# Split SiLU-multiply: loads on SP, stores on ACT, and one wide activation and multiply per tile

## The chip, the cores and the metric

One core of one Trainium2 chip runs the kernel. The metric is the device time of one execution in microseconds (us), as a median over runs. A page or a trace shows one profiled execution; its span is about 2 us shorter than the device time of the same execution (468.9 against 470.65 us for the kernel before).

Engines: ACT is ScalarE, DVE is VectorE, SP is SyncE, which here only issues transfers. A "q" after the name (SPq, ACTq, DVEq) means that engine's sequencer. 16 DMA engines move the data.

## The reference

```python
def setup_inputs():
    batch, seq, dim = (32, 512, 2048)
    return {'x': np.random.randn(batch, seq, dim).astype(np.float32)}

def reference(x):
    half_dim = x.shape[-1] // 2
    x1, x2 = (x[..., :half_dim].copy(), x[..., half_dim:].copy())
    silu_x1 = x1 * (1 / (1 + np.exp(-x1)))
    return (silu_x1 * x2).astype(np.float32)
```

134.22 MB have to be read and 67.11 MB written. Per element of output there is one SiLU and one multiply.

## The kernel before

The 16384 rows are cut into 16 tiles of 1024 rows. Each of the 128 partitions holds 8 rows of a tile, so a load is 8.39 MB and a store 4.19 MB. There are two input buffers and two output buffers. Tile i+2 can be loaded only when the last multiply of tile i has read its input.

```python
K = 8
KC = 2
in_pool  = ...tile_pool(name="in_pool", bufs=2)
out_pool = ...tile_pool(name="out_pool", bufs=2)
# ... cut ...
def load(i):
    xt = in_pool.tile([P, K, in_cols], dt, name="xt")
    nc.scalar.dma_start(out=xt[:, :plan[i][1], :], in_=view(x_flat, i))   # loads: ACT queue
    loaded[i] = xt

load(0)
load(1)
for i in range(n_tiles):
    # ... cut ...
    for c in range(0, k, KC):                     # 4 chunks of 2 rows
        ce = min(c + KC, k)
        nc.scalar.activation(out=ot[:, c:ce, :], in_=xt[:, c:ce, :half], func=Silu)
        nc.vector.tensor_mul(out=ot[:, c:ce, :], in0=ot[:, c:ce, :], in1=xt[:, c:ce, half:])
        if last:
            nc.sync.dma_start(out=ov[:, c:ce, :], in_=ot[:, c:ce, :])      # stores: SP queue
    if not last:
        nc.sync.dma_start(out=ov, in_=ot[:, :k, :])
    if i + 2 < n_tiles:
        load(i + 2)
```

With four chunks, the activation of one chunk runs beside the multiply of the chunk before.

Of the kernel before, what the change touches and what calls it, by code (L numbers as in the profile page):

```python
# [1 line left out]

# [4 lines left out]


def issue_ahead_of_the_first_barrier(nc):




    head, body = nc.main_func.blocks[:2]
    load = next(ins for ins in body.instructions if type(ins).__name__ == "InstDMACopy")
    at = next(
        j for j, ins in enumerate(head.instructions)
        if ins.engine == load.engine and type(ins).__name__ == "InstDrain"
    )
    body.instructions = [ins for ins in body.instructions if ins.name != load.name]  # L20
    head.instructions = head.instructions[:at] + [load] + head.instructions[at:]


@with_exitstack
def kernel(
    ctx: ExitStack,
    tc: tile.TileContext,
    x: bass.AP,
    out: bass.AP,
):  # L30






    nc = tc.nc
    P = nc.NUM_PARTITIONS

    x_flat = x.flatten_outer_dims()  # L40
    out_flat = out.flatten_outer_dims()
    num_rows, in_cols = x_flat.shape
    half = in_cols // 2
    dt = x_flat.dtype

    K = 8
    KC = 2
    PLAN = [K] * (num_rows // (P * K))

    in_pool = ctx.enter_context(tc.tile_pool(name="in_pool", bufs=2))  # L50
    out_pool = ctx.enter_context(tc.tile_pool(name="out_pool", bufs=2))

    plan = []
    row = 0
    for k in PLAN:
        plan.append((row, k))
        row += P * k
    assert row == num_rows
    n_tiles = len(plan)

    def view(flat, i):
        row0, k = plan[i]
        return flat[row0:row0 + P * k].rearrange("(p k) d -> p k d", k=k)

    nc.at_finalize(issue_ahead_of_the_first_barrier)


    ctx.enter_context(tc.manual_schedule())

    loaded = {}  # L70

    def load(i):
        xt = in_pool.tile([P, K, in_cols], dt, name="xt")
        nc.scalar.dma_start(out=xt[:, :plan[i][1], :], in_=view(x_flat, i))
        loaded[i] = xt

    load(0)
    load(1)
    for i in range(n_tiles):
        k = plan[i][1]  # L80
        xt = loaded.pop(i)
        last = i == n_tiles - 1
        ov = view(out_flat, i)
        ot = out_pool.tile([P, K, half], dt, name="ot")
        for c in range(0, k, KC):
            ce = min(c + KC, k)
            nc.scalar.activation(  # L87
                out=ot[:, c:ce, :],
                in_=xt[:, c:ce, :half],
                func=mybir.ActivationFunctionType.Silu,  # L90
            )
            nc.vector.tensor_mul(  # L92
                out=ot[:, c:ce, :],
                in0=ot[:, c:ce, :],
                in1=xt[:, c:ce, half:],
            )
            if last:
                nc.sync.dma_start(out=ov[:, c:ce, :], in_=ot[:, c:ce, :])
        if not last:
            nc.sync.dma_start(out=ov, in_=ot[:, :k, :])  # L100
        if i + 2 < n_tiles:
            load(i + 2)


# [1 line left out]
_INS = ['x']  # L106
_OUTS = [((32, 512, 1024), 'float32')]


# [23 lines left out]
```

## Time and profile before

| | before |
|---|---|
| device time, median of 3 runs before the prediction | 470.82 us |
| bytes moved, mean rate | 201.35 MB, 429 GB/s |
| DVE busy, ACT busy | 30%, 25% |
| from arrival of a tile's load to the issue of its store and of the next load but one | 10.87 us |
| arrival to arrival | 29.0 us |

These lines are from the page of the kernel before. In part 3, a row is a queue with its packets, its bytes, and its packets' time as a share of 16 engines' span. In part 5, the columns are busy time and mean length of one instruction, then the idle time before and its releaser. In part 6, the last column is the median time from issue to landing.

```profile
span 468.9 us, 269 instructions
DVE 142.3 (30%) x64; ACT 118.2 (25%) x65; POOL 0.2 (0%) x4
q10 hardware_dynamic: 2304, 134.22, 66.4%
q1 hardware_dynamic: 2736, 67.11, 33.2%
...
DMA xt<-in_x_dram 80%; DVE ot L92 15%; ACT ot L87 3%; DVEq L128 0%
...
L92 DVE TENSOR_TENSOR ot<-ot,xt 128x2048 f32<-128x2048 f32 x64 | 142.3, 2286 | 319.5 <-ACT ot L87 319.5
L87 ACT ACTIVATE ot<-xt 128x2048 f32<-128x2048 f32 x64 | 116.9, 1897 | 338.8 <-DMA xt<-in_x_dram 338.8
...
out_dram<-ot SPq DMA_DIRECT2D x15, 4096.0 KB, 39.8
xt<-in_x_dram ACTq DMA_DIRECT2D x16, 47.1
```

The two queues' packets fill 66.4 + 33.2 = 99.6% of the 16 engines' time. Compute engines stand idle most of the time, waiting for a load.

Three rows of the table by stretches follow. The columns are the stretch in us, its length, busy time of DVE, ACT and POOL, the clock, the DMA share and GB/s. The first two rows are two tiles each in the middle; the last is part of the finish, after the last load has arrived. A packet is counted whole in the stretch in which it starts, so short stretches scatter around 434 GB/s.

```profile
44.50:102.60 58.10, 17.79 (x8) 14.62 (x8) 0.00 (x0) 1.00 1.00 433
102.60:160.60 58.00, 17.79 (x8) 14.63 (x9) 0.00 (x0) 1.00 1.00 434
...
455.00:458.00 3.00, 3.00 (x3) 3.00 (x2) 0.00 (x0) 1.00 0.76 325
```

This is one link of the chain of waits, in order of time (start, length, what):

```profile
44.54 1.92 ACT ot L87
...
46.48 8.91 DVE ot L92 x4
...
55.41 47.19 DMA xt<-in_x_dram
```

The load is on the chain for 47.19 us. A tile of 12.58 MB (8.39 in, 4.19 out) takes only 29.0 us at 434 GB/s. For the other 18 us that load stood behind the load issued before it.

The finish, in order of time (start, length, what):

```profile
451.03 7.31 ACT L87 ACTIVATE ot<-xt 128x2048 f32<-128x2048 f32 x4 [21.57 <-DMA xt<-in_x_dram]
455.29 6.94 SPq L98 DMA_DIRECT2D out_dram<-ot  x4
```

Stores of the last tile start leaving 4.26 us after its arrival. What is left of the store before them covers that time.

### The profile page before, as it was taken

The page shows a single profiled execution, that of the slowest core. Times are in us where ns is not written, and L with a number is a line of the kernel's source. Part 1 is how long each engine was busy: PE and PEld are TensorE (multiplying, and loading weights), DVE is VectorE, ACT ScalarE, POOL GpSimd, SP SyncE. Part 2 cuts the span into 40 slices and gives each one's busy share as a digit, 9 for nine tenths or more (in the row PEclk, how much of TensorE's full clock was granted, in tenths as well). Part 3 has the DMA queues.
Part 4 walks back from the last instruction along what each step waited for, and adds up shares of the span by engine and source line. Part 5 has one row for each costly group of instructions (what it writes and reads, how often), then busy time and mean ns, then how long its engine had stood idle before and what let it go on. Part 6 is the DMA issues. An engine that isn't in the chain of part 4 may idle for free.

```text
span 468.9 us, 269 instructions
## 1 busy us (share of the span) xinstructions
DVE 142.3 (30%) x64; ACT 118.2 (25%) x65; POOL 0.2 (0%) x4
## 2 busy tenths in 40 slices
DVE  0070705106061160601507025070250702407034
ACT  1142406023060330603206032060420604106051
POOL 0000000000000000000000000000000000000000
DMA  9899999999999998999999999999999989999998
GB/s 431 375 447 403 447 447 447 403 419 431 447 447 403 447 492 363 442 492 391 458 403 439 456 447 403 409 442 447 447 403 444 467 386 447 442 419 481 400 409 354
DMA packets 5042, 201.35 MB, mean 429 GB/s; under 512 B 560, under 2 KB 560, under 8 KB 560
## 3 DMA queue, kind: packets, MB, share of 16 engines
q10 hardware_dynamic: 2304, 134.22, 66.4%
q1 hardware_dynamic: 2736, 67.11, 33.2%
q14 instruction: 2, 0.02, 0.0%
HBM read 134.22 MB, written 67.11 MB: 429 GB/s over the span
## 4 chain that ended last, share of the span: by engine, by line
DMA 80%; DVE 15%; ACT 3%; DVEq 0%; issue 0%
DMA xt<-in_x_dram 80%; DVE ot L92 15%; ACT ot L87 3%; DVEq L128 0%
## 5 line engine op out<-in xcount | busy, mean ns | idle before, releaser
L92 DVE TENSOR_TENSOR ot<-ot,xt 128x2048 f32<-128x2048 f32 x64 | 142.3, 2286 | 319.5 <-ACT ot L87 319.5
L87 ACT ACTIVATE ot<-xt 128x2048 f32<-128x2048 f32 x64 | 116.9, 1897 | 338.8 <-DMA xt<-in_x_dram 338.8
L87 ACT ACT_TABLE_LOAD x1 | 1.3, 1283 | 1.3 <-PEq L117 1.3
L117 POOL MEMSET const-uint8-127<- 128x1 uint8 x1 | 0.1, 102 | 0.0
L117 POOL MEMSET const-bfloat16-1.0<- 128x1 bf16 x1 | 0.1, 101 | 0.0
L117 POOL MEMSET const-float32-0.0<- 128x1 f32 x1 | 0.1, 98 | 0.2 <-issue 0.2
L117 POOL MEMSET const-float32-1.0<- 128x1 f32 x1 | 0.1, 98 | 0.0
## 6 DMA issues: line engine op xcount, KB each, us to landing
out_dram<-ot SPq DMA_DIRECT2D x15, 4096.0 KB, 39.8
out_dram<-ot SPq DMA_DIRECT2D x4, 1024.0 KB, 5.7
xt<-in_x_dram ACTq DMA_DIRECT2D x16, 47.1
```

What stands on the lines that cost most here:

```text
L87: nc.scalar.activation(out=ot[:, c:ce, :], in_=xt[:, c:ce, :half], func=mybir.ActivationFunctionType.Silu,)
L92: nc.vector.tensor_mul(out=ot[:, c:ce, :], in0=ot[:, c:ce, :], in1=xt[:, c:ce, half:],)
L117: nc = _bacc.Bacc("TRN2", target_bir_lowering=False, num_devices=1)
```

## The change

The intent is fewer, larger instructions: one activation and one multiply over all 8 rows in tiles 1 to 14, so 22 of each instead of 64. The queues are exchanged: loads go out from SP, stores from ACT. Tiles 0 and 15 keep chunks of 2 rows. In the last tile the store of a chunk stands two chunks behind in ACT's program, so that its wait for the multiply does not hold back the next activations.

```diff
-        nc.scalar.dma_start(out=xt[:, :plan[i][1], :], in_=view(x_flat, i))
+        nc.sync.dma_start(out=xt[:, :plan[i][1], :], in_=view(x_flat, i))
 # ... cut: silu() and mul() wrap the same activation and multiply ...
-        for c in range(0, k, KC):
-            # activation, tensor_mul of 2 rows; in the last tile a store of 2 rows on nc.sync
-        if not last:
-            nc.sync.dma_start(out=ov, in_=ot[:, :k, :])
-        if i + 2 < n_tiles:
-            load(i + 2)
+        if i < n_tiles - 1:
+            kc = KC_EDGE if i == 0 else K
+            for c in range(0, K, kc):
+                silu(ot, xt, c, c + kc)
+                mul(ot, xt, c, c + kc)
+            nc.scalar.dma_start(out=ov, in_=ot)
+            if i + 2 < n_tiles:
+                load(i + 2)
+            continue
+        cuts = list(range(0, K, KC_EDGE))
+        for n, c in enumerate(cuts + [None, None]):
+            if c is not None:
+                silu(ot, xt, c, c + KC_EDGE)
+                mul(ot, xt, c, c + KC_EDGE)
+            if n >= 2:
+                b = cuts[n - 2]
+                nc.scalar.dma_start(out=ov[:, b:b + KC_EDGE, :], in_=ot[:, b:b + KC_EDGE, :])
```

More of the change, by code (lines that the diff above doesn't have):

```diff
@@ L46 @@
     K = 8
-    KC = 2
+    KC_EDGE = 2
     PLAN = [K] * (num_rows // (P * K))
@@ L73, in load, with silu, mul @@
         xt = in_pool.tile([P, K, in_cols], dt, name="xt")
-        nc.scalar.dma_start(out=xt[:, :plan[i][1], :], in_=view(x_flat, i))
+        nc.sync.dma_start(out=xt[:, :plan[i][1], :], in_=view(x_flat, i))
         loaded[i] = xt
+    def silu(ot, xt, c, ce):
+        nc.scalar.activation(
+            out=ot[:, c:ce, :],
+            in_=xt[:, c:ce, :half],
+            func=mybir.ActivationFunctionType.Silu,
+        )
+    def mul(ot, xt, c, ce):
+        nc.vector.tensor_mul(
+            out=ot[:, c:ce, :],
+            in0=ot[:, c:ce, :],
+            in1=xt[:, c:ce, half:],
+        )
     load(0)
@@ L79 @@
     for i in range(n_tiles):
-        k = plan[i][1]
         xt = loaded.pop(i)
-        last = i == n_tiles - 1
         ov = view(out_flat, i)
         ot = out_pool.tile([P, K, half], dt, name="ot")
-        for c in range(0, k, KC):
-            ce = min(c + KC, k)
-            nc.scalar.activation(
-                out=ot[:, c:ce, :],
-                in_=xt[:, c:ce, :half],
-                func=mybir.ActivationFunctionType.Silu,
-            )
-            nc.vector.tensor_mul(
-                out=ot[:, c:ce, :],
-                in0=ot[:, c:ce, :],
-                in1=xt[:, c:ce, half:],
-            )
-            if last:
-                nc.sync.dma_start(out=ov[:, c:ce, :], in_=ot[:, c:ce, :])
-        if not last:
-            nc.sync.dma_start(out=ov, in_=ot[:, :k, :])
-        if i + 2 < n_tiles:
-            load(i + 2)
+        if i < n_tiles - 1:
[15 more added lines that the diff above has]
+                nc.scalar.dma_start(out=ov[:, b:b + KC_EDGE, :], in_=ot[:, b:b + KC_EDGE, :])
 _INS = ['x']
```

## The prediction

> **What bounds the kernel now.** The 16 DMA engines, over the whole span. The queue table shows 134.22 MB loaded and 67.11 MB stored, 429 GB/s over the 468.9 us span; the stretches between the arrivals of odd-numbered loads (chain of waits: every 58.0 us) moved 433 to 434 GB/s at a DMA share of 1.00. DVE is busy 30% and ACT 25%. The chain of waits gives compute 18%, but it is not exposed: while tile i is computed (10.9 us), load i+1 and an older store keep the engines full. The Trainium skill, "DMA: Bandwidth & Descriptors", section "Where 436 GB/s comes from", gives 435 GB/s as the ceiling of the 16 ports; the trace's 434 agrees. 201.3 MB at 434 GB/s is 464 us.
>
> **The slack.** Loads arrive every 29.05 us. A load is issued 10.9 us after the arrival two before it, 18.1 us before its predecessor has landed. A store takes 39.8 us from issue to landing, 10.7 more than the period: when it is issued the store queue still holds about 10.7 us of the store before.
>
> **What the change does.**
> 1. Tiles 1 to 14: one activation of 128x8192, then one multiply of 128x8192, no longer overlapped. Measured: 1.893 us per activation of 2048 columns, 2.284 us per multiply. The skill, "ScalarE: Activation LUTs", section "What ACT_TABLE_LOAD costs", gives 186 ns + 0.833 ns per column, which is 1.892 us at 2048 and so agrees; at 8192 it gives 7.01 us. The multiply by a similar split (estimate, 0.15 us fixed plus four times the rest): 8.7 us. So load to issue goes from 10.9 to 15.7 us, 4.8 later.
> 2. The delay fits into the slack of both queues: 18.1 to 13.3 us for loads, 10.7 to 5.9 us for stores. Neither runs dry, so loads still arrive every 29.05 us. Issue to landing should shrink by the same 4.8 us: loads 47.1 to about 42.3, stores 39.8 to about 35.0.
> 3. Swapping the queues moves the waits to other sequencers; issues cost 0.33 to 0.37 us each, all hidden. At the start the first load leaves from SP instead of ACT: within 0.3 us.
> 4. Last tile: before, its first store is issued 4.3 us after the last load landed (451.0 to 455.3), and the remains of store 14 (about 2.5 MB after 451 us, 6 us) cover that. Now this store stands behind three activations on ACT (about 5.7 us) and may leave up to 1.5 us later, while store 14 has no more left than before: 0 to 1.3 us of DMA idleness, say 0.3.
>
> **On the critical path:** only step 4 and the start. I expect 471.0 us, 80% range 470.0 to 472.3: the same within 2%.
>
> **Right or wrong.** Step 1: one activation near 7.0 us, one multiply near 8.7, in the groups. Step 2: median landings 42 and 35 us; arrivals every 29.05 us; DMA share 1.00 in the middle. Step 4: first store of the last tile 4.3 to 5.8 us after the last arrival; DMA gap before it at most 1.5 us.
>
> **What would make it wrong:** the two queues not sharing alike once swapped; store 14 finishing before the last tile's stores start; a different rate for another mixture of reads and writes. Each is worth a few us at most, so more than 9 us either way is very unlikely.

## The result, and the profile after

| | before | after |
|---|---|---|
| device time, median (range) of 6 runs each | 470.94 (470.62 to 471.61) us | 470.64 (470.44 to 471.34) us |
| ratio after/before, 95% interval | | 0.9994 (0.9981 to 1.0007) |
| span of the profiled run | 468.9 us | 468.6 us |
| arrival to issue, tiles 1 to 14 | 10.87 us | 15.78 us |
| arrival to arrival | 29.0 us | 29.0 us |

A ratio in this document is the mean time of one kernel's fast runs over that of the other's of the same rounds, so it is not quite the ratio of the medians quoted. Executions over 1.5% slower than the fastest of the same kernel are left out of the means. The result is the same time: the interval includes 1.

The page after, the same lines:

```profile
span 468.6 us, 183 instructions
DVE 139.5 (30%) x22; ACT 114.3 (24%) x23; POOL 0.2 (0%) x4
q1 hardware_dynamic: 2304, 134.22, 66.4%
q10 hardware_dynamic: 2736, 67.11, 33.2%
...
DMA xt<-in_x_dram 72%; DVE ot L85 14%; ACT ot L78 11%; DVEq L140 0%; ACTq L78 0%
...
out_dram<-ot ACTq DMA_DIRECT2D x15, 4096.0 KB, 34.7
xt<-in_x_dram SPq DMA_DIRECT2D x16, 42.1
```

Busy time fell by 2.8 us on DVE and 3.9 us on ACT, and nothing came of it. Landings fell by the 5 us by which the issues came later. On the chain of waits compute rose from 18% to 25%, about 33 us more, in the same total time: a share of the chain is not a cost.

Lengths of single instructions (shortest, median, longest in ns) by the tile view of the output:

```profile
L78 ACT ACTIVATE ot<-xt x22: 1893/7029/7029, 21.8 to 456.1; 128x8192 f32<-128x8192 f32 x14, 128x2048 f32<-128x2048 f32 x8
L85 DVE TENSOR_TENSOR ot<-ot,xt x22: 2283/8691/8693, 23.8 to 459.3; 128x8192 f32<-128x8192 f32 x14, 128x2048 f32<-128x2048 f32 x8
```

The same stretches, and one link of the chain:

```profile
44.50:102.60 58.10, 17.38 (x2) 14.06 (x2) 0.00 (x0) 1.00 1.00 433
102.60:160.60 58.00, 17.39 (x2) 14.06 (x2) 0.00 (x0) 1.00 1.00 434
...
455.00:458.00 3.00, 3.00 (x2) 3.00 (x2) 0.00 (x0) 1.00 0.78 333
```

```profile
44.84 7.04 ACT ot L78
...
51.90 8.70 DVE ot L85
...
60.62 42.14 DMA xt<-in_x_dram
```

The link now has 15.8 us of compute and 42.1 us of load, where it had 10.9 and 47.2. Its sum, 58.0 us for two tiles, has not moved, and neither have the DMA share of 1.00 and the 433 to 434 GB/s.

The finish, in order of time:

```profile
450.73 5.51 ACT L78 ACTIVATE ot<-xt 128x2048 f32<-128x2048 f32 x3 [21.93 <-DMA xt<-in_x_dram]
...
455.00 0.34 ACTq L114 DMA_DIRECT2D out_dram<-ot  x1
456.15 1.89 ACT L78 ACTIVATE ot<-xt 128x2048 f32<-128x2048 f32 x1
```

The first store left 4.27 us after the arrival, against 4.26 before. It left while the third activation was still running (until 450.73 + 5.51 = 456.24 us): the sequencer does not wait for the activations ahead of the store to finish. The Trainium skill, "Perfetto Trace Analysis", section "Sequencer Loop", says that a sequencer pushes engine instructions into a queue and reads on; this trace agrees.

### The profile page after: what moved, and what is told of

It is laid out like the page before. It is cut to its first block, busy times and chain, and to the rows that moved or that the text cites. A ratio compares the mean times of both kernels' runs of the same rounds, so it can differ in the third digit from the quotient of the medians.

```text
span 468.6 us, 183 instructions
## 1 busy us (share of the span) xinstructions
DVE 139.5 (30%) x22; ACT 114.3 (24%) x23; POOL 0.2 (0%) x4
## 3 DMA queue, kind: packets, MB, share of 16 engines
q1 hardware_dynamic: 2304, 134.22, 66.4%
## 4 chain that ended last, share of the span: by engine, by line
DMA 72%; DVE 14%; ACT 11%; DVEq 0%; issue 0%; ACTq 0%
DMA xt<-in_x_dram 72%; DVE ot L85 14%; ACT ot L78 11%; DVEq L140 0%; ACTq L78 0%
## 5 line engine op out<-in xcount | busy, mean ns | idle before, releaser
L85 DVE TENSOR_TENSOR ot<-ot,xt 128x8192 f32<-128x8192 f32 (+1 forms) x22 | 139.5, 6362 | 322.1 <-ACT ot L78 322.1
L78 ACT ACTIVATE ot<-xt 128x8192 f32<-128x8192 f32 (+1 forms) x22 | 113.0, 5163 | 343.0 <-DMA xt<-in_x_dram 343.0
## 6 DMA issues: line engine op xcount, KB each, us to landing
out_dram<-ot ACTq DMA_DIRECT2D x15, 4096.0 KB, 34.7
xt<-in_x_dram SPq DMA_DIRECT2D x16, 42.1
```

## The experiments

The main theory, "slack": the DMA engines set the time, and arrival to issue may grow a good deal in the middle for nothing; only start and finish count. The rivals were "chain" (compute between arrival and issue costs its length in each two-tile link, and something hides that) and "two effects cancel" (one part of the change gains what the other loses). All kernels ran beside runs of the kernel before on the same chip. The runs were made in four batches, each on another chip of the same kind (swap_only, wide_only, act_x2 and act_x3; thin and the three of start and finish; act_x2h and act_x4; act_x2q); the kernel before took 470.8 to 471.0 us on all four. Medians in the summary are of 4 runs, or 5 for the first two; those of act_x2 and act_x3 include one slow run each. The second and third columns are read from each profiled run; that of act_x3 alone counts as slow. The second is counted from the start of a tile's first activation, the third is a mean over tiles in the middle.

| kernel | arrival to issue | us a tile | time, us | before, us | ratio to before (95%) |
|---|---|---|---|---|---|
| swap_only | 10.9 | 29.0 | 471.05 | 470.99 | 1.0002 (0.9990 to 1.0015) |
| wide_only | 15.8 | 29.0 | 471.59 | 470.99 | 1.0008 (0.9995 to 1.0020) |
| thin (wrong result) | 2.3 | 29.0 | 471.53 | 470.98 | 1.0012 (0.9997 to 1.0027) |
| act_x2 | 22.8 | 29.0 | 470.90 | 470.99 | 0.9996 (0.9978 to 1.0014) |
| act_x2q | 24.8 | 30.5 | 494.66 | 471.00 | 1.0506 (1.0489 to 1.0524) |
| act_x2h | 26.5 | 31.3 | 501.52 | 470.81 | 1.0633 (1.0590 to 1.0675) |
| act_x3 | 29.9 | 31.9 | 513.72 | 470.99 | 1.0864 (1.0806 to 1.0922) |
| act_x4 | 37.0 | 37.4 | 592.73 | 470.81 | 1.2585 (1.2564 to 1.2606) |
| first_wide | 15.8 | 29.0 | 471.19 | 470.98 | 1.0003 (0.9988 to 1.0018) |
| last_wide | 15.8 | 29.0 | 480.75 | 470.98 | 1.0208 (1.0191 to 1.0225) |
| no_lag | 15.8 | 29.0 | 475.83 | 470.98 | 1.0105 (1.0090 to 1.0120) |

### The two parts alone

swap_only takes the changed kernel and keeps chunks of 2 rows in all tiles:

```diff
-            kc = KC_EDGE if i == 0 else K
+            kc = KC_EDGE
```

> Loads on SP, stores on ACT and the last tile's order as after, but small ops everywhere. Slack theory: load to issue stays 10.9 us, landings stay 47 us (loads) and 39.7 us (stores), time within 0.6 us of before (470.9). Rival 'two effects cancel' (the queue swap gains what the wide ops lose): faster than before by 2 us or more.

Measured: ratio 1.0002, landings 47.0 us (loads) and 39.6 us (stores):

```profile
out_dram<-ot ACTq DMA_DIRECT2D x15, 4096.0 KB, 39.6
...
xt<-in_x_dram SPq DMA_DIRECT2D x16, 47.0
```

The exchange of queues alone does nothing. The Trainium skill, "DMA: Bandwidth & Descriptors", section "Issuing engines are not separate DMA queues", says that transfers from either engine run on the same 16 DMA engines and interleave; this run agrees.

wide_only takes the kernel before, with its queues and its last tile, and makes tiles 1 to 14 wide:

```diff
-        for c in range(0, k, KC):
-            ce = min(c + KC, k)
+        kc = KC if i == 0 or last else K      # KC is 2, K is 8
+        for c in range(0, k, kc):
+            ce = min(c + kc, k)
```

> Wide activation and multiply in tiles 1 to 14, queues and last tile as before. Slack theory: landings 42.1 and 34.7 us as after, loads still 29.0 us apart, time within 0.6 us of before. Rival 'the chain of waits is right': 4.8 us later in each of its seven two-tile links is slower by up to 34 us. Rival 'two effects cancel': slower than before by 2 us or more.

Measured: ratio 1.0008, landings 42.2 and 34.7 us:

```profile
out_dram<-ot SPq DMA_DIRECT2D x15, 4096.0 KB, 34.7
...
xt<-in_x_dram ACTq DMA_DIRECT2D x16, 42.2
```

Two effects that cancel are ruled out at the size of 2 us: each part alone is within 0.2% of the kernel before at the far end of its interval. The chain's 34 us are ruled out as well.

### Compute almost taken away

thin makes all transfers of the changed kernel but computes 128 of 1024 columns. Both output tiles are filled with zeros once at the start. Its output is wrong, which doesn't matter for the time.

```diff
+    ots = [...]                 # two output tiles, memset to 0.0, reused as ots[i % 2]
-            out=ot[:, c:ce, :], in_=xt[:, c:ce, :half], func=Silu
+            out=ot[:, c:ce, :THIN], in_=xt[:, c:ce, :THIN], func=Silu      # THIN = 128
-            out=ot[:, c:ce, :], in0=ot[:, c:ce, :], in1=xt[:, c:ce, half:]
+            out=ot[:, c:ce, :THIN], in0=ot[:, c:ce, :THIN], in1=xt[:, c:ce, half:half + THIN]
```

> All transfers of the changed kernel, but only 128 of 1024 columns are computed (wrong result on purpose; the out tiles are filled with zeros once at the start): arrival to issue about 3 us instead of 15.8. Slack theory: nothing to gain, the transfers alone take this time: within 1 us of after, load landings about 55 us after issue. Rival 'compute is on the chain': about 13 us less in each of seven links, 80 us or more faster.

Measured: ratio 1.0012; arrivals every 29.0 us; loads land 55.6 us after issue. One stretch of two tiles and the loads:

```profile
102.60:160.60 58.00, 2.45 (x2) 2.11 (x2) 0.00 (x0) 1.00 1.00 433
```

```profile
xt<-in_x_dram SPq DMA_DIRECT2D x16, 55.6
```

With 2.3 us instead of 15.8 between arrival and issue, the loads only wait longer behind each other. This is the most direct evidence for the bound: with DVE busy for 34 us (20 of multiplies, 14 of fills) instead of 139, the time is the same. The rate in the middle was 433 to 434 GB/s with full and with almost no compute. The Trainium skill, "SBUF — State Buffer", section "Who interferes with whom", says that DMA never contends with a compute engine, and nothing here speaks against it.

### More compute: where does the slack end?

The changed kernel with its wide activation repeated into the same place, so that the result stays correct. act_x2, act_x3 and act_x4 run it 2, 3 and 4 times:

```diff
                 silu(ot, xt, c, c + kc)
+                if i > 0:
+                    for _ in range(1):           # range(2), range(3) in act_x3, act_x4
+                        silu(ot, xt, c, c + kc)
                 mul(ot, xt, c, c + kc)
```

> The changed kernel with each wide activation of tiles 1 to 14 run twice (same values, result unchanged): arrival to issue 15.8 + 6.9 = 22.7 us. Slack theory: still under the 29.0 us between arrivals, so loads never starve; the store queue (5.7 us of backlog) runs dry, which costs nothing while loads flow: within 1 us of after, loads landing about 35 us after issue. Rival 'chain': 7 links of 6.9 us, about 48 us slower.

Measured: ratio 0.9996, though ACT was busy for 213 us instead of 114. Loads landed 35.0 us after issue, as expected. The chain theory's 48 us did not appear. The store queue did run dry once, at the start (the first store landed at 66.5 us, the second was issued at 67.9 us), at no cost. In act_x2, act_x2q, act_x2h and first_wide most activations wait last for the store of two tiles before, which must leave its output buffer first and lands about 0.2 us after the load; more output buffers were not tried. One of the four runs took 486.2 us, at an undiminished clock. It counts as slow, was not profiled, and stays unexplained; whether act_x2 stands so near the end of the slack that it sometimes loses time is not shown.

> Each wide activation run three times: arrival to issue 29.6 us, just over the 29.0 us between arrivals. Slack theory: the knee is passed; in every second tile both queues run dry for some us. Estimate from 434 GB/s, two thirds to loads, 2 us to start a transfer: about 27 us slower than after (10 to 40), DMA share visibly under 1 in the middle. Rival 'chain': about 97 us slower.

Measured: 513.72 us; the three fast runs are 41 us over before, just outside the expected 10 to 40. (The 2 us to start a transfer are an estimate. For scale: load 0 of the kernel before landed 21.7 us after its issue, where 8.39 MB take 19.3 us at 434 GB/s.) The four runs scatter from 507.81 to 517.59 us, and the profiled one counts as slow, so its trace is not used for causes. Past the knee, the estimate was too small. Two further kernels look at that part of the curve. act_x2h adds to act_x2 an activation over 4 rows, act_x2q one over 2 rows:

```diff
+                    silu(ot, xt, c, c + kc)
+                    silu(ot, xt, 0, K // 2)      # K // 4 in act_x2q
```

> The changed kernel with each wide activation of tiles 1 to 14 run once more on all 8 rows and once on 4: arrival to issue about 26.3 us, 2.7 us ahead of the next arrival at full rate. Theory A, a transfer needs only about 2 us to start (as estimated before act_x3): no loss, within 1 us of before. Theory B, act_x3 showed pairs of transfers issued 1 to 4 us ahead landing 32.5 to 35 us later instead of 29, so about 5 us of lead are needed: 1.2 us lost in each of 14 tiles, 10 to 20 us slower.

Measured: 501.52 us, 31 us slower. Theory A falls; theory B has the right sign but expected 10 to 20.

> Between act_x2 (22.8 us from arrival to issue, no loss) and act_x2h (26.4 us, 30 us slower): one more activation on 2 of 8 rows, 24.6 us. Naive slack (a load must be issued 2 us before its predecessor lands at 29.05): within 1 us of before. Theory B' (about 6 us of lead are needed, less lead costs up to 2.3 us a tile, and a longer period gives lead back): about 1 us lost per tile, 10 to 18 us slower.

Measured: 494.66 us, 24 us slower; naive slack falls, and B' again expected too little. So the slack ends between 22.8 and 24.8 us of arrival to issue, and at once by 1.5 us a tile. These are the queues and one stretch, first of act_x2, then of act_x2q:

```profile
q1 hardware_dynamic: 2304, 134.22, 66.4%
q10 hardware_dynamic: 2736, 67.11, 33.2%
...
160.60:218.60 58.00, 17.38 (x2) 28.11 (x5) 0.00 (x0) 1.00 1.00 434
```

```profile
q1 hardware_dynamic: 2304, 134.22, 67.2%
q10 hardware_dynamic: 2736, 67.11, 31.6%
...
160.60:218.60 58.00, 15.38 (x2) 31.93 (x6) 0.00 (x0) 1.00 1.00 407
```

The DMA share is still 1.00, but at 407 GB/s. Times the span, the load packets took 66.4% of 468.9 = 311 us in act_x2 and 67.2% of 492.2 = 331 us in act_x2q; the store packets 156 us in both. So most of the loss of 23 us shows as slower load packets, about 20 / 14 = 1.4 us for each load, and not as idle engines. The mean lead does not explain it: the next pair of transfers is issued 29.0 - 22.8 = 6.2 us before the pair ahead lands in act_x2, and 30.5 - 24.8 = 5.7 us in act_x2q.

The packets and completion signals in the packed traces show a little more. Not every load packet is slow: the median of the 2048 large ones is 2.42 us in both runs, but 567 of them took over 2.5 us in act_x2q and 33 in act_x2, and two thirds of the time lost in this way falls into the 8 us after a load was issued. A load ends with 16 completion signals. In act_x2 the last comes 0.3 to 0.8 us after the first; in act_x2q it is 2.7 to 5.0 us from load 3 on, the load that was issued only 1.4 us before the one ahead had landed (3.5 us in act_x2). If each signal stands for one DMA engine, then the engine that is done first has about 3 us less lead than the figure above, so that lead stays a possible cause. Why the packets slow down there stays open.

> Each wide activation run four times: arrival to issue about 36.6 us. Theory: beyond the knee only the chain of issue, landing and compute counts, two tiles per round, so each further us of compute costs half a us per tile: 6.9 x 14 / 2 = 48 us over act_x3, 85 to 97 us slower than before. If compute were simply added (not shared by two buffers): 97 us over act_x3.

Measured: 592.73 us, 122 us slower than before, where 85 to 97 were expected: a miss. Over the fast runs of act_x3 it is 81 us, between the 48 and the 97 of the two theories. A wait that they had left out shows in the timeline:

```profile
82.44 28.21 ACT L78 ACTIVATE ot<-xt 128x8192 f32<-128x8192 f32 x4 [9.22 <-DVE ot L85]
...
119.87 28.21 ACT L78 ACTIVATE ot<-xt 128x8192 f32<-128x8192 f32 x4 [9.22 <-DVE ot L85]
```

The activations of a tile start only after the multiply of the tile before, 37.43 us after their predecessors, although they need none of its data (the load for the second line had landed at 114.5 us): in ACT's program the store stands between them and waits for that multiply. Activation, multiply and store issue are then serial, and that sum is the period. No run tried to part them.

### Start and finish

first_wide makes the first tile wide too:

```diff
-            kc = KC_EDGE if i == 0 else K
+            kc = K
```

> The changed kernel with the first tile wide too: its store and the third load are issued at 37.6 instead of 32.7 us. Slack theory: load 1 alone has work until about 41 us, so nothing starves: within 0.6 us of after. Rival 'the edges need small chunks': up to 4.8 us slower.

Measured: ratio 1.0003. The small chunks of the first tile are not needed: store 0 and load 2 left at 37.66 us instead of 32.70, while load 1 kept the engines busy until it landed at 41.2 us.

last_wide makes the last tile wide too, with one store:

```diff
-        if i < n_tiles - 1:
+        if True:
```

> The changed kernel with the last tile wide too and stored in one piece. Slack theory: here nothing is left to load, so the delay is exposed: the store is issued 15.8 us after the last arrival (466.5 us), while the rest of store 14 ends about 6 us after it, so the engines idle about 10 us and then move 4.2 MB: 11 us slower than after (9 to 13). A theory by which wide ops never matter: no difference.

Measured: 480.75 us, 9.8 us slower than before. The store left at 466.77 us, 15.8 us after the arrival, and needed 11.1 us to land:

```profile
450.98 7.03 ACT L78 ACTIVATE ot<-xt 128x8192 f32<-128x8192 f32 x1 [21.86 <-DMA xt<-in_x_dram]
...
466.77 0.34 ACTq L102 DMA_DIRECT2D out_dram<-ot  x1
```

The lengthening that is free in tiles 1 to 14 is paid in the last tile.

no_lag issues each store of the last tile right after its multiply:

```diff
-        for n, c in enumerate(cuts + [None, None]):
+        for n, c in enumerate(cuts):
-            if n >= 2:
-                b = cuts[n - 2]
+            if True:
+                b = cuts[n]
```

> The changed kernel, in whose last tile each store is issued right after its multiply, not two chunks later; the store's wait on ACT then holds back the next activation. Slack theory: chunks no longer overlap, stores are issued 4.3, 8.5, 12.7, 16.9 us after the last arrival instead of 4.3 to 10.9: about 5 us slower than after (4 to 6). If ACT's sequencer ran ahead of a waiting store: no difference.

Measured: 475.83 us, 4.9 us slower than before. The timeline of the last tile shows why:

```profile
454.93 0.34 ACTq L114 DMA_DIRECT2D out_dram<-ot  x1
455.31 1.91 ACT L78 ACTIVATE ot<-xt 128x2048 f32<-128x2048 f32 x1 [2.74 <-DVE ot L85]
...
468.88 0.34 ACTq L114 DMA_DIRECT2D out_dram<-ot  x1
```

Each activation now waits 2.74 us for the multiply before it, because the store in front of it waits for that multiply. The last store leaves at 468.88 us; in the changed kernel its DMA is issued by 461.94. So with stores on ACT, a lag is needed to keep the finish as it was with stores on SP; whether one chunk would do was not tried.

None of the runs pointed to a version that beats both kernels. 201.3 MB at 434 GB/s is 464 us of a span of 468.6, and start and finish share the rest.

## Why the prediction was right

471.0 us was predicted (470.0 to 472.3), and 470.64 us measured.

1. Bound: right. The middle runs at DMA share 1.00 and 433 to 434 GB/s in both kernels. thin shows that the transfers alone take this time.
2. Step 1, size of the delay: right. The activation is 7.029 us (predicted 7.0, which was an estimate), the multiply 8.691 us (8.7), arrival to issue 15.78 us (15.7).
3. Step 2, the delay fits into the slack: right. Landings are 42.1 and 34.7 us (predicted 42.3 and 35.0), arrivals still every 29.0 us, and wide_only alone is the same. But "18.1 to 13.3 us for loads" was too generous. It took all time until the next arrival as slack. act_x2 could spend 7 us more and lose nothing in its fast runs; act_x2q spent 9 us more and lost 24 us. The usable rest was 7 to 9 us, not 13.3.
4. Step 3, queues and start: right. swap_only's ratio is 1.0002; the first arrival came at 21.83 us after, 21.88 before.
5. Step 4, the finish: the 0.3 us added for it were wrong. It took the first store as standing behind three finished activations (about 5.7 us). It left after 4.27 us, while the third still ran. The engines' share from 455 to 458 us was 0.78, before 0.76, so no gap was added.

The 0.3 us by which the median after is lower lie inside the interval, and neither part alone shows them. They are not explained and need no explanation.

## What to carry to other kernels

Here the DMA engines ran at 433 to 434 GB/s through the middle of the kernel, and neither fewer compute instructions nor another issuing queue moved the time. In such a kernel ask first how long the engines would still have queued work if compute took longer, and test that by repeating an instruction, as act_x2 did. Here the slack was shorter than the time until the next arrival, and it ended abruptly. The last tile had no such slack: small chunks saved 9.8 us there, and stores that hold back no compute 4.9 us.

## What the Trainium skill lacked or had wrong

- No page gives how far ahead of its predecessor's landing a load must be issued to keep the full rate; the place would be "DMA: Bandwidth & Descriptors". Here issuing 22.8 us after an arrival kept 434 GB/s, and 24.8 us dropped to about 410 GB/s with the engines still shown as busy.
- "DMA: Bandwidth & Descriptors", section "Anatomy of one DMA — SWDGE (gpsimd) path", fits about 2.0 us plus size over 436 GB/s for transfers issued from GpSimd. Lone stores issued from ACT needed less: 11.1 us for 4.19 MB (last_wide) and 3.9 us for 1.05 MB (no_lag), which is about 1.5 us over size at 434 GB/s.
